# A two-block network on one core: its first transfers in smaller parts, its last sum in PSUM

## The chip, the cores and the metric

The kernel runs on one core of one Trainium2 chip. The metric is device time in microseconds (us) of one execution; the median of several runs counts. The engines are TensorE (PE in the rows, its weight loads PEld), VectorE (DVE), ScalarE (ACT), GpSimd (POOL) and SyncE (SP, which here only issues transfers; SPq and ACTq are the issuing instructions of the two queues).

## The reference, cut to what matters

Two transformer-like blocks are applied to x, which has 256 tokens of 1024 features, all in float32. The change touches the first operation and the last ones.

```python
def first_block(x, norm_mix_pre, w_in, ...):
    h = rms_norm(x, norm_mix_pre[l])
    proj = h @ w_in[l]                 # the first product: 1024 x 5376
    ...                                # attention, a delta-rule recurrence, gates, a gated FFN

def second_block(x, mem, ...):
    ...                                # a mixer and an attention over mem, each added to x
    x = x + squared_relu_mlp(rms_norm_2(x, g_mlp), w_up, w_down)   # 1024 -> 4096 -> 1024
    return rms_norm_2(x, g_final)

def squared_relu_mlp(h, w_up, w_down):
    a = jax.nn.relu(h @ w_up)
    return (a * a) @ w_down
```

`rms_norm(x, g)` is x * rsqrt(mean(x^2) + 1e-6) * g over the features.

## The kernel before

**Layout.** Activations lie feature-major: 128 partitions by 8 chunks of 256 tokens. Every large product keeps float32 accuracy by splitting both factors into a part that the matmul takes exactly (hi) and a rest (lo), and summing three products: hi*hi, hi*lo and lo*hi.

**Weights.** They stream from memory in slabs of 128 partitions by 1024 numbers (512 KB). `slab` issues one transfer on SP's queue into `wraw` (3 buffers), ScalarE copies it to `whi` (line 182) and VectorE subtracts to get `wlo` (line 183; 4 buffers each). A `wraw` buffer is free for the next transfer when that subtraction is done, so SP often stands waiting for VectorE. `plan` lists the slabs in order; `fetch(ahead)` starts slabs until so many are ready, and `next_slab` calls `fetch(AHEAD)`, with AHEAD = 3, each time TensorE takes one. One slab gives 24 matmuls of 256 columns. `block` and `group` are the loops over a 256-column group (line 247); `mm` (line 262) is the plain matmul.

**Start.** Function `first` loads x in two halves of 512 KB on SP's queue, with the first slab between them, and the small vectors `vec` on ScalarE's queue. The products of the first three groups of `w_rw` do not wait for the norm: `scaled` (lines 314 and 315) makes `gh` and `gl`, which are x times the gain without the norm, and the factor `r` = rsqrt(mean square) of each token comes in when the PSUM banks are read (`shifted`, lines 485 and 487). `rstd` makes r: squares on ScalarE (line 275), sums on VectorE (279 and 330), a matmul with ones (`ssum`), then Ln and Exp on ScalarE (line 145). All later groups use `xh` and `xl`, the normed input, which `normed` makes on VectorE and ScalarE (lines 338, 266 and 267). Constants for the attention mask (`sbf`, line 760) are loaded on ScalarE's queue and cast to bf16 (`sbm`, line 762).

**End.** Function `mlp` works on x without its norm (relu squared lets the factor out), so the product that w_down gives is scaled by r^2 of the token. `norm` makes r2 by token. `turned` transposes the gain g_final and x itself to token-major (lines 1307 and 1315) beside the up product. `tokens` multiplies token-major with 512 columns: two feature halves g, and in each the 16 slabs in order, every slab for both token halves t. Then, for each (g, t), VectorE makes y = ps * r2 + x (line 1338), ScalarE squares y with a sum (line 1340) and VectorE multiplies by the gain (1341). When both halves are there, r of the last norm is made by token and the result scaled (1350 and 1352) and written by four transfers on SP's queue (line 1353).

**Order.** The source order is a priority. A planner simulates the engines with costs of its own and fixes one order of instructions for each engine and queue; on the chip each of them goes strictly in that order. An instruction of low priority may so stand early, as a filler, where the planner expected a gap.

Of the kernel before, what the change touches and what calls it, by code (L numbers as in the profile page):

```python
# [17 lines left out]
P = 128  # L18
# [73 lines left out]
class Net:  # L92
# [47 lines left out]

    def table(self, name):
        self._chain(self.nc.scalar.preload_act_table_set(name))
# [26 lines left out]
    def fetch(self, ahead):  # L169
        while self.queue and len(self.ready) < ahead:  # L170
            name, i = self.queue.pop(0)
            self.ready.append((name, i, self.slab(name, i)))

    def slab(self, name, i):
        nc = self.nc
        off, k0, m, c0 = slabs(*WEIGHTS[name])[i]
        w = m * width(name)
        raw = self.pr.tile([P, SW], F32, tag="wraw", name="wraw")
        hi = self.ph.tile([P, SW], F32R, tag="whi", name="whi")
        lo = self.pl.tile([P, SW], F32R, tag="wlo", name="wlo")  # L180
        nc.sync.dma_start(raw[:, :w], self.io[name][off:off + P * w].rearrange("(p n) -> p n", p=P))
        nc.scalar.copy(hi[:, :w], raw[:, :w])  # L182
        nc.vector.tensor_sub(lo[:, :w], raw[:, :w], hi[:, :w].bitcast(F32))  # L183
        h3 = hi[:, :w].rearrange("p (k c) -> p k c", k=m)
        l3 = lo[:, :w].rearrange("p (k c) -> p k c", k=m)
        return h3, l3, k0, m
# [18 lines left out]
    def tokens(self, name, g, xh, xl):  # L205

        banks = [self.bank().rearrange("p c t -> p (c t)") for _ in range(2)]
        per, count = blocks(name), WEIGHTS[name][0] // P
        for b in range(per):
            hi, lo, k0, m = self.next_slab(name, g * per + b)  # L210
            for t, ps in enumerate(banks):
                tt = slice(t * P, (t + 1) * P)
                for k in range(m):
                    kk = k0 + k
                    for i, (a, w) in enumerate(((xh, hi), (xh, lo), (xl, hi))):
                        self.mm(ps, a[:, kk, tt], w[:, k, :], start=kk == 0 and i == 0,
                                stop=kk == count - 1 and i == 2)
        return banks
# [199 lines left out]
def first(n):  # L418
    nc, tc = n.nc, n.tc
    with ExitStack() as ctx:  # L420
# [15 lines left out]
        for i in range(2):  # L436
            nc.sync.dma_start(xin[i].rearrange("p c t -> p (c t)"), n.io["x"][:, i * 1024:(i + 1) * 1024])
            n.fetch(1)
        nc.scalar.dma_start(n.vec, n.io["vec"])
        n.table("natural_log_exp_and_others")  # L440
        xp = pairs(xin[0]) + pairs(xin[1])
# [4 lines left out]
        n.scaled(xp, "norm_mix_pre", gh, gl)  # L446
        r = n.rstd(tmp, xp, D, "rs")
        n.fetch(AHEAD)
# [22 lines left out]
        def shifted(g, dst, d0, scale=None, swapped=False):  # L471
            if scale is None:
                ps = n.group("w_rw", g, n.xh, n.xl)
            else:
                ps = n.group("w_rw", g, gh, gl, ps=n.sx("rw").rearrange("p (c t) -> p c t", c=2))
# [20 lines left out]
        nc.sync.dma_start(n.cst, n.io["cst"][:, :NRES])  # L496
# [263 lines left out]
        nc.scalar.dma_start(sbf, n.io["cst"][:, o:o + w])  # L760
# [529 lines left out]
def mlp(n, tmp, out):  # L1290
    nc, tc = n.nc, n.tc
    with ExitStack() as ctx:
# [3 lines left out]
        r2 = pool.tile([P, 2], F32, name="r2")  # L1296
        xt = pool.tile([P, 2, D], F32, name="xt")

        def norm():
            n.rstd_tok(pool, [n.squares(tmp, pairs(n.x))], D, square=r2)  # L1300

        def turned():

            for f in range(2):
                pt = n.ax("turn")
                for i in range(4):
                    nc.tensor.transpose(pt[:, i * P:(i + 1) * P],
                                        n.v("g_final_2", 4 * f + i).to_broadcast([P, P]), n.c("ident"))
                nc.scalar.copy(gf[:, f * 512:(f + 1) * 512], pt)
                yield  # L1310
            for t in range(2):
                for f in range(2):
                    pt = n.ax("turn")
                    for i in range(4):
                        nc.tensor.transpose(pt[:, i * P:(i + 1) * P],
                                            n.x[:, 4 * f + i, t * P:(t + 1) * P], n.c("ident"))
                    nc.scalar.copy(xt[:, t, f * 512:(f + 1) * 512], pt)
                    yield
# [15 lines left out]
        for g in range(2):  # L1334
            gg = slice(g * 512, (g + 1) * 512)
            for t, ps in enumerate(n.tokens("w_down_2", g, ah, al)):
                y = xt[:, t, gg]
                nc.vector.scalar_tensor_tensor(y, ps, r2[:, t:t + 1], y, op0=ALU.mult, op1=ALU.add)
                sq = tmp.tile([P, 512], F32, tag="t2", name="sq", bufs=n.t2)
                nc.scalar.activation(sq, y, AF.Square, accum_out=st[:, t, g:g + 1])  # L1340
                nc.vector.tensor_mul(o[:, t, gg], y, gf[:, gg])
        for t in range(2):
            s = st[:, t, :]
            nc.vector.tensor_add(s[:, 2:3], s[:, 0:1], s[:, 1:2])
            n.act(s[:, 3:4], s[:, 2:3], AF.Ln, bias=n.eps, scale=1.0 / D)
            n.act(s[:, 3:4], s[:, 3:4], AF.Exp, scale=-0.5)
            for f in range(2):
                oo = o[:, t, f * 512:(f + 1) * 512]
# [4 lines left out]
                nc.sync.dma_start(out[t * P:(t + 1) * P, f * 512:(f + 1) * 512], oo)  # L1353
# [85 lines left out]
```

## Time and profile before

| | |
|---|---|
| median of 3 runs | 851.95 us (851.76 to 854.29) |
| profiled execution, its own time | 853.44 us |
| its span, first to last instruction | 851.7 us |
| mean granted TensorE clock | 0.994 of full speed |
| TensorE busy | 829.5 us, 97% of the span |
| VectorE busy | 565.3 us, 66% |
| ScalarE busy | 464.9 us, 55% |
| moved by transfers | 142.88 MB, 168 GB/s over the span |

Line numbers (L247) are lines of the kernel before. In a timeline row the first number is the start and the second the duration in us; "x4" are instructions merged into one row; in square brackets stands how long the engine was idle before it and what ended that. A busy TensorE is not one at its peak, as matmuls are pipelined: what one costs is read from the distance between starts.

### The profile page before, as it was taken

The numbers are of one execution on the slowest core, as the hardware profiler recorded it, in microseconds if no ns is written. First come the engines' busy times: TensorE is split into PE (matmuls) and PEld (weight loads), VectorE is DVE, ScalarE is ACT, GpSimd is POOL, SyncE is SP. The second block draws the span as 40 slices with busy tenths as digits, with TensorE's granted clock in tenths as the row PEclk, the third lists the DMA queues.
The fourth block names the chain that finished last, engine by engine and source line by source line (L and its number), as shares of the span: only waits on it lengthen the run. The fifth ranks groups of instructions, "written<-read, shape, count | busy, mean of one in ns | idle before, by whom it ended". The sixth has DMA issues, their size and how long they took to land.

```text
span 851.7 us, 15759 instructions
## 1 busy us (share of the span) xinstructions
PE 829.5 (97%) x6508; PEld 788.4 (93%) x6508; DVE 565.3 (66%) x790; ACT 464.9 (55%) x714; POOL 5.4 (1%) x14
## 2 busy tenths in 40 slices
PE   5999998999999999999999999999999999999996
PEld 5798987999999999999999998999999999988884
DVE  6858689455888776666545876689576666654543
ACT  6497355643577654445445657457455565553432
POOL 0001001000000000000000000000000000000000
PEclk9999999999999999999999999999999999999999
DMA  8434443542464765555555564455524555556551
GB/s 283 149 133 159 136 130 117 160 140 87 145 251 144 225 189 183 195 177 197 173 187 186 158 202 149 148 174 184 188 95 153 176 172 177 193 178 193 179 193 50
DMA packets 44631, 142.88 MB, mean 168 GB/s; under 512 B 8976, under 2 KB 9744, under 8 KB 44304
## 3 DMA queue, kind: packets, MB, share of 16 engines
q1 hardware_dynamic: 43840, 139.25, 50.7%
q10 hardware_dynamic: 720, 2.63, 0.8%
q8 instruction: 51, 0.84, 0.4%
q14 instruction: 20, 0.16, 0.1%
HBM read 139.17 MB, written 2.69 MB: 167 GB/s over the span
## 4 chain that ended last, share of the span: by engine, by line
PE 90%; DVE 5%; DMA 2%; ACT 2%; issue 1%; SPq 0%; ACTq 0%; DVEq 0%
PE mm L247 68%; PE mm L262 11%; DMA wraw<-in_w_rw 2%; PE pz L262 2%; DVE wlo L183 1%; PE po L262 1%; ACT whi L182 1%; PE px L262 1%; PE mgnh L262 1%; PE nv L262 1%; DVE prw L736 1%; PE kv L247 1%; PE ssum L262 1%; DVE pr L718 1%; DVE TF L719 0%
## 5 line engine op out<-in xcount | busy, mean ns | idle before, releaser
L183 DVE TENSOR_TENSOR wlo<-wraw,whi 128x1024 fp32r<-128x1024 f32 x254 | 308.2, 1215 | 198.8 <-ACT whi L182 197.3
L182 ACT CAST whi<-wraw 128x1024 fp32r<-128x1024 f32 x254 | 264.8, 1044 | 291.5 <-PE mm L247 174.9
L247 PE MATMUL mm<-xh,whi 128*128 128x256 f32 x1120 | 319.3, 285 | 0.0
L247 PE MATMUL mm<-xh,wlo 128*128 128x256 f32 x1120 | 316.1, 282 | 1.8 <-DVE wlo L183 1.8
L247 PE MATMUL mm<-xl,whi 128*128 128x256 f32 x1120 | 316.1, 282 | 0.0
L247 PEld LDWEIGHTS mm<-xh,whi 128*128 128x128 f32 x1120 | 212.0, 189 | 3.8 <-issue 2.2
L247 PEld LDWEIGHTS mm<-xh,wlo 128*128 128x128 f32 x1120 | 211.8, 189 | 2.9 <-DVE wlo L183 2.2
L247 PEld LDWEIGHTS mm<-xl,whi 128*128 128x128 f32 x1120 | 211.8, 189 | 0.9 <-issue 0.7
L262 PE MATMUL mm<-whi,ah 128*128 128x512 f32 x128 | 50.6, 395 | 0.0
L262 PE MATMUL mm<-whi,al 128*128 128x512 f32 x128 | 50.6, 395 | 0.0
L262 PE MATMUL mm<-wlo,ah 128*128 128x512 f32 x128 | 50.6, 395 | 0.0
L247 PE MATMUL mm<-fh,whi 128*128 128x256 f32 x176 | 49.1, 279 | 0.0
L247 PE MATMUL mm<-fl,whi 128*128 128x256 f32 x176 | 49.1, 279 | 0.0
L247 PE MATMUL mm<-fh,wlo 128*128 128x256 f32 x176 | 49.1, 279 | 0.0
L247 PEld LDWEIGHTS mm<-fl,whi 128*128 128x128 f32 x176 | 33.1, 188 | 0.0
L247 PEld LDWEIGHTS mm<-fh,wlo 128*128 128x128 f32 x176 | 33.1, 188 | 0.0
L247 PEld LDWEIGHTS mm<-fh,whi 128*128 128x128 f32 x176 | 33.1, 188 | 0.0
L262 PEld LDWEIGHTS mm<-whi,al 128*128 128x128 f32 x128 | 24.1, 188 | 5.8
L262 PEld LDWEIGHTS mm<-wlo,ah 128*128 128x128 f32 x128 | 24.1, 188 | 5.8
L262 PEld LDWEIGHTS mm<-whi,ah 128*128 128x128 f32 x128 | 24.1, 188 | 5.7
L247 PE MATMUL rw<-gh,whi 128*128 128x256 f32 x48 | 14.2, 296 | 9.0 <-ACT whi L182 9.0
L247 PE MATMUL mm<-memh,whi 128*128 128x256 f32 x64 | 18.8, 294 | 0.0
(349 smaller groups left out, 1379.9 us busy)
## 6 DMA issues: line engine op xcount, KB each, us to landing
wraw<-in_w_up SPq DMA_DIRECT2D x32, 512.0 KB, 3.5
wraw<-in_w_down SPq DMA_DIRECT2D x32, 512.0 KB, 4.3
wraw<-in_w_in SPq DMA_DIRECT2D x24, 512.0 KB, 4.2
wraw<-in_w_ffn_gate SPq DMA_DIRECT2D x22, 512.0 KB, 3.8
wraw<-in_w_ffn_up SPq DMA_DIRECT2D x22, 512.0 KB, 3.3
wraw<-in_w_ffn_down SPq DMA_DIRECT2D x20, 512.0 KB, 3.5
wraw<-in_w_gate SPq DMA_DIRECT2D x16, 512.0 KB, 3.3
wraw<-in_w_kv_mem SPq DMA_DIRECT2D x16, 512.0 KB, 3.3
```

What stands on the lines that cost most here:

```text
L182: nc.scalar.copy(hi[:, :w], raw[:, :w])
L183: nc.vector.tensor_sub(lo[:, :w], raw[:, :w], hi[:, :w].bitcast(F32))
L247: self.nc.tensor.matmul(ps[:, c, :], lhsT, rhs, start=first, stop=last, skip_group_check=True)
L262: self.nc.tensor.matmul(out, lhsT, rhs, start=start, stop=stop, skip_group_check=True)
L718: nc.vector.tensor_mul(pr[:, :, :, :t + 1], tri[:, :, :, :t + 1], q)
L736: nc.vector.tensor_mul(pr, left[:, r:r + 4, :].rearrange("p r (o i) -> p r o i", o=1).to_broadcast([P, 4, 16, 16]), right.rearrange("p (o ...
```

## The change

It has two halves. **At the start**, x comes in three transfers on two queues (256 KB on SP's, then 256 KB and 512 KB on ScalarE's, behind `vec`), the first slab comes in two transfers with its copies in two parts, TensorE multiplies ones by ones 12 times into a bank that nobody reads, and the source order is changed: a quarter of x, the first slab, the second quarter, the second slab, the rest of x, the third slab, the first product group, and only then `rstd`. The mask constants go on SP's queue, behind `cst`. **At the end**, the residual is summed by TensorE in the banks of the last product. As a norm follows, the sum may be scaled by token: x * ms + f, with ms = mean(x^2) + eps, replaces x + f * r^2, and the last norm's eps is scaled by ms^2. So x is multiplied by ms in place (four VectorE instructions), `norm` has one more matmul, the transposes of x and line 1338 are gone, and `residual` adds 16 float32 matmuls against the identity, four to each bank, ahead of the bank's slabs. In the second feature half the last two slabs are held back and gone through by token half, and the output leaves on two queues.

```diff
-    def fetch(self, ahead):
+    def fetch(self, ahead, parts=1):
...
+        cols = [slice(q * w // parts, (q + 1) * w // parts) for q in range(parts)]
+        for c in cols:
+            nc.sync.dma_start(raw[:, c], src[:, c])
+        for c in cols:
+            nc.scalar.copy(hi[:, c], raw[:, c])
+            nc.vector.tensor_sub(lo[:, c], raw[:, c], hi[:, c].bitcast(F32))
...
-    def tokens(self, name, g, xh, xl):
+    def tokens(self, name, g, xh, xl, first, hold=0):
...
+        for t, ps in enumerate(banks):
+            first(g, t, ps)
+
+        def part(slab, t):
+            hi, lo, k0, m = slab
+            tt = slice(t * P, (t + 1) * P)
+            for k in range(m):
+                kk = k0 + k
+                for i, (a, w) in enumerate(((xh, hi), (xh, lo), (xl, hi))):
+                    self.mm(banks[t], a[:, kk, tt], w[:, k, :], start=False, stop=kk == count - 1 and i == 2)
+
+        for b in range(per - hold):
+            slab = self.next_slab(name, g * per + b)
+            for t in range(2):
+                part(slab, t)
+        held = [self.next_slab(name, g * per + b) for b in range(per - hold, per)]
+        for t in range(2):
+            for slab in held:
+                part(slab, t)
...
-        for i in range(2):
-            nc.sync.dma_start(xin[i].rearrange("p c t -> p (c t)"), n.io["x"][:, i * 1024:(i + 1) * 1024])
-            n.fetch(1)
         nc.scalar.dma_start(n.vec, n.io["vec"])
+        for i, (queue, q) in enumerate(((nc.sync, 0), (nc.scalar, 2), (nc.scalar, 4))):
+            w = 2 if i < 2 else 4
+            dst = xin[q // 4][:, q % 4:q % 4 + w, :].rearrange("p c t -> p (c t)")
+            queue.dma_start(dst, n.io["x"][:, q * T:(q + w) * T])
         n.table("natural_log_exp_and_others")
+
+        idle = n.ax("idle")
+        for i in range(12):
+            n.mm(idle[:, :P], n.ones, n.ones)
...
-        n.scaled(xp, "norm_mix_pre", gh, gl)
+        n.scaled(xp[:1], "norm_mix_pre", gh, gl)
+        n.fetch(1, parts=2)
+        n.scaled(xp[1:2], "norm_mix_pre", gh, gl, 1)
+        n.fetch(2)
+        n.scaled(xp[2:], "norm_mix_pre", gh, gl, 2)
+        n.fetch(AHEAD)
+        rw = {}
+
+        def raw_group(g):
+            rw[g] = n.group("w_rw", g, gh, gl, ps=n.sx("rw").rearrange("p (c t) -> p c t", c=2))
+
+        raw_group(0)
         r = n.rstd(tmp, xp, D, "rs")
-        n.fetch(AHEAD)
...
-        nc.sync.dma_start(n.cst, n.io["cst"][:, :NRES])
+        cst = nc.sync.dma_start(n.cst, n.io["cst"][:, :NRES])
...
-        nc.scalar.dma_start(sbf, n.io["cst"][:, o:o + w])
+        n.after(nc.sync.dma_start(sbf, n.io["cst"][:, o:o + w]), cst)
...
         def norm():
-            n.rstd_tok(pool, [n.squares(tmp, pairs(n.x))], D, square=r2)
+            sq = n.squares(tmp, pairs(n.x))
+            ps, pr = n.ax("ssum"), n.ax("rtok")
+            n.mm(ps[:, :T], n.ones, sq)
+            for t in range(2):
+                n.mm(pr[:, t:t + 1], sq[:, t * P:(t + 1) * P], n.ones[:, 0:1], start=t == 0)
+            nc.vector.tensor_scalar(ms, ps[:, :T], 1.0 / D, EPS, op0=ALU.mult, op1=ALU.add)
+            nc.vector.tensor_scalar(epsm, pr[:, :2], 1.0 / D, EPS, op0=ALU.mult, op1=ALU.add)
+            nc.vector.scalar_tensor_tensor(epsm, epsm, EPS, epsm, op0=ALU.mult, op1=ALU.mult)
+            for x in pairs(n.x):
+                nc.vector.tensor_mul(x, x, pair(ms))
...
-            for t in range(2):
-                for f in range(2):
-                    pt = n.ax("turn")
-                    for i in range(4):
-                        nc.tensor.transpose(pt[:, i * P:(i + 1) * P],
-                                            n.x[:, 4 * f + i, t * P:(t + 1) * P], n.c("ident"))
-                    nc.scalar.copy(xt[:, t, f * 512:(f + 1) * 512], pt)
-                    yield
+
+        def residual(f, t, ps):
+            for i in range(4):
+                n.mm(ps[:, i * P:(i + 1) * P], n.x[:, 4 * f + i, t * P:(t + 1) * P], n.c("ident"),
+                     start=i == 0)
...
-            for t, ps in enumerate(n.tokens("w_down_2", g, ah, al)):
-                y = xt[:, t, gg]
-                nc.vector.scalar_tensor_tensor(y, ps, r2[:, t:t + 1], y, op0=ALU.mult, op1=ALU.add)
+            for t, ps in enumerate(n.tokens("w_down_2", g, ah, al, residual, hold=2 * g)):
                 sq = tmp.tile([P, 512], F32, tag="t2", name="sq", bufs=n.t2)
-                nc.scalar.activation(sq, y, AF.Square, accum_out=st[:, t, g:g + 1])
-                nc.vector.tensor_mul(o[:, t, gg], y, gf[:, gg])
+                nc.scalar.activation(sq, ps, AF.Square, accum_out=st[:, t, g:g + 1])
+                nc.vector.tensor_mul(o[:, t, gg], ps, gf[:, gg])
...
-            n.act(s[:, 3:4], s[:, 2:3], AF.Ln, bias=n.eps, scale=1.0 / D)
+            n.act(s[:, 3:4], s[:, 2:3], AF.Ln, bias=epsm[:, t:t + 1], scale=1.0 / D)
...
-                nc.sync.dma_start(out[t * P:(t + 1) * P, f * 512:(f + 1) * 512], oo)
+                (nc.sync if f else nc.scalar).dma_start(out[t * P:(t + 1) * P, ff], oo)
```

## Rows read from the trace of the kernel before

**Rows 1.** The page, part 1: busy time of each engine over the span.

```profile
PE 829.5 (97%) x6508; PEld 788.4 (93%) x6508; DVE 565.3 (66%) x790; ACT 464.9 (55%) x714; POOL 5.4 (1%) x14
```

**Rows 2.** Waits of TensorE, whole span: in total, times, longest, us.

```profile
PE rw L247 <- ACT whi L182: 9.0, 1, 9.0
...
PE mm L247 <- DVE wlo L183: 1.8, 1, 1.8
```

**Rows 3.** Busy time by stretch; last columns: granted clock, DMA share, GB/s.

```profile
23.00:33.00 10.00, 8.51 (x61) 6.94 (x59) 9.58 (x18) 5.59 (x9) 0.00 (x0) 1.00 0.34 106
...
756.00:842.70 86.70, 86.70 (x373) 69.88 (x372) 38.68 (x35) 31.19 (x33) 0.00 (x0) 1.00 0.51 160
```

**Rows 4.** Timeline of VectorE, start of the kernel.

```profile
6.55 1.68 DVE L315 SCALAR_TENSOR_TENSOR gl<-x,vec,gh 128x256 fp32r<-128x256 f32 x4 [0.29 <-ACT gh L314]
...
8.96 1.23 DVE L183 TENSOR_TENSOR wlo<-wraw,whi 128x1024 fp32r<-128x1024 f32 x1 [0.73 <-ACT whi L182]
...
15.95 0.42 DVE L330 TENSOR_TENSOR sqa<-sqa 128x256 f32<-128x256 f32 x1
...
18.15 0.49 DVE L485 SCALAR_TENSOR_TENSOR wx<-rw,omu,rs 128x256 f32<-128x256 f32 x1 [0.65 <-ACT rs L145]
...
23.17 1.22 DVE L183 TENSOR_TENSOR wlo<-wraw,whi 128x1024 fp32r<-128x1024 f32 x1 [1.23 <-ACT whi L182]
...
30.18 1.90 DVE L267 TENSOR_TENSOR xl<-nh,xh 128x512 fp32r<-128x512 f32 x3 [0.24 <-ACT xh L266]
32.00 2.35 DVE L183 TENSOR_TENSOR wlo<-wraw,whi 128x1024 fp32r<-128x1024 f32 x2
```

**Rows 5.** Timeline of ScalarE, start of the kernel.

```profile
6.01 1.70 ACT L314 ACTIVATE gh<-x,vec 128x256 fp32r<-128x256 f32 x4 [3.55 <-DMA vec<-in_vec]
7.88 1.04 ACT L182 CAST whi<-wraw 128x1024 fp32r<-128x1024 f32 x1 [0.17 <-DMA wraw<-in_w_rw]
...
15.44 0.51 ACT L762 CAST sbm<-sbf 128x384 bf16<-128x384 f32 x1
...
17.19 0.47 ACT L145 ACTIVATE lg<-ssum,eps 128x256 f32<-128x256 f32 x1 [1.05 <-PE ssum L262]
```

**Rows 6.** Single microseconds of the start, columns as in rows 3.

```profile
4.00:5.00 1.00, 0.00 (x0) 0.00 (x0) 0.00 (x0) 0.00 (x0) 0.00 (x0) 1.00 0.91 241
...
10.00:11.00 1.00, 0.76 (x3) 0.76 (x4) 1.00 (x3) 1.00 (x3) 0.00 (x0) 1.00 0.42 168
11.00:12.00 1.00, 1.00 (x7) 1.00 (x6) 1.00 (x4) 1.00 (x3) 0.00 (x0) 1.00 0.78 184
...
18.00:19.00 1.00, 1.00 (x11) 1.00 (x11) 0.85 (x3) 0.98 (x2) 0.00 (x0) 1.00 0.93 340
...
34.00:35.00 1.00, 1.00 (x6) 1.00 (x6) 1.00 (x3) 0.00 (x0) 0.00 (x0) 0.50 0.67 147
```

**Rows 7.** The chain that ended last, in order of time: pieces of TensorE.

```profile
45.07 1.73 PE gpre L262 x8
46.80 1.78 PE cum L262 x16
...
690.23 0.44 PE turn L1315 x4
```

**Rows 8.** Timeline of the last microseconds, VectorE, ScalarE and SP's queue.

```profile
844.11 0.75 DVE L1338 SCALAR_TENSOR_TENSOR xt<-mm,r,xt 128x512 f32<-128x512 f32 x1
...
844.90 0.63 ACT L1340 ACTIVATE sq<-xt 128x512 f32<-128x512 f32 x1 [0.67 <-DVE xt L1338]
...
845.95 0.28 ACT L145 ACTIVATE fst<-fst,eps 128x1 f32<-128x1 f32 x1
...
846.74 0.19 ACT L145 ACTIVATE fst<-fst 128x1 f32<-128x1 f32 x1
846.96 0.72 ACT L1352 ACTIVATE o<-o,fst 128x512 f32<-128x512 f32 x1
...
846.59 1.96 SPq L1353 DMA_DIRECT2D out<-o  x4
```

More of the change, by code (lines that the diff above doesn't have):

```diff
@@ L139, in _chain, with after @@
         self.last_table = ins.ins
+    def after(self, ins, other):
+        self.tc.add_manual_dep(
+            ins.ins, other.ins.name,
+            mybir.DependencyInfo(mybir.DependencyClass.NoSync, mybir.DependencyReason.DATA),
+            reason="transfers in order")
     def table(self, name):
@@ L167, in plan_together, with slab @@
             self.queue += [(name, g * blocks(name) + b) for name, g in groups]
-    def fetch(self, ahead):
+    def fetch(self, ahead, parts=1):
         while self.queue and len(self.ready) < ahead:
             name, i = self.queue.pop(0)
-            self.ready.append((name, i, self.slab(name, i)))
-    def slab(self, name, i):
+            self.ready.append((name, i, self.slab(name, i, parts)))
+    def slab(self, name, i, parts=1):
         nc = self.nc
@@ L180, in slab @@
         lo = self.pl.tile([P, SW], F32R, tag="wlo", name="wlo")
-        nc.sync.dma_start(raw[:, :w], self.io[name][off:off + P * w].rearrange("(p n) -> p n", p=P))
-        nc.scalar.copy(hi[:, :w], raw[:, :w])
-        nc.vector.tensor_sub(lo[:, :w], raw[:, :w], hi[:, :w].bitcast(F32))
+        src = self.io[name][off:off + P * w].rearrange("(p n) -> p n", p=P)
+        cols = [slice(q * w // parts, (q + 1) * w // parts) for q in range(parts)]
[4 more added lines that the diff above has]
+            nc.vector.tensor_sub(lo[:, c], raw[:, c], hi[:, c].bitcast(F32))
         h3 = hi[:, :w].rearrange("p (k c) -> p k c", k=m)
@@ L203, in together @@
         return banks
-    def tokens(self, name, g, xh, xl):
+    def tokens(self, name, g, xh, xl, first, hold=0):
         banks = [self.bank().rearrange("p c t -> p (c t)") for _ in range(2)]
         per, count = blocks(name), WEIGHTS[name][0] // P
[L209 to L217, printed above, removed]
+        for t, ps in enumerate(banks):
[15 more added lines that the diff above has]
+                part(slab, t)
         return banks
@@ L474, in shifted @@
             else:
-                ps = n.group("w_rw", g, gh, gl, ps=n.sx("rw").rearrange("p (c t) -> p c t", c=2))
+                if g not in rw:
+                    raw_group(g)
+                ps = rw[g]
             t = pad[g % 2]
@@ L1295, in mlp @@
         gf = pool.tile([P, D], F32, name="gf")
-        r2 = pool.tile([P, 2], F32, name="r2")
-        xt = pool.tile([P, 2, D], F32, name="xt")
+        ms = pool.tile([P, T], F32, name="ms")
+        epsm = pool.tile([P, 2], F32, name="epsm")
         def norm():
-            n.rstd_tok(pool, [n.squares(tmp, pairs(n.x))], D, square=r2)
+            sq = n.squares(tmp, pairs(n.x))
[8 more added lines that the diff above has]
+                nc.vector.tensor_mul(x, x, pair(ms))
         def turned():
@@ L1344, in mlp @@
             nc.vector.tensor_add(s[:, 2:3], s[:, 0:1], s[:, 1:2])
-            n.act(s[:, 3:4], s[:, 2:3], AF.Ln, bias=n.eps, scale=1.0 / D)
+            n.act(s[:, 3:4], s[:, 2:3], AF.Ln, bias=epsm[:, t:t + 1], scale=1.0 / D)
             n.act(s[:, 3:4], s[:, 3:4], AF.Exp, scale=-0.5)
             for f in range(2):
-                oo = o[:, t, f * 512:(f + 1) * 512]
+                ff = slice(f * 512, (f + 1) * 512)
+                oo = o[:, t, ff]
                 if f:
```

## The prediction

> **What bounds the kernel now.** I read the page first. TensorE is busy for 829.5 of 851.7 us [rows 1], so an edit can win only in the few stretches where TensorE stands, and whatever it adds to TensorE elsewhere is paid in full. The view of TensorE's waits says where it stands [rows 2]: 9.0 us until the first slab is copied, and 1.8 us for a `wlo`; to these comes the tail behind its last matmul. The change works at exactly these places: at the first two with its first half, at the tail with the first part of its second half.
>
> Next come the stretches of the start. From 23 to 33 us VectorE is busy for 9.58 of 10 us, TensorE for 8.51 [rows 3]. The timeline of VectorE shows why. It starts on `gl` at 6.55, and the `wlo` for which TensorE waits is the first of the two that start at 32.00; two take 2.35 us, so it is there at about 33.2 [rows 4]. In the 26.65 us between, VectorE waits only four times: 0.73, 0.65, 1.23 and 0.24 us [rows 4], 2.85 us together. The other 23.8 us are work, mostly without a gap. So the start is not bound by TensorE, and not by the transfers alone: it is a queue of 23.8 us of VectorE's work that must be gone through before the first product of the normed input can go on. The reader should keep this ledger in mind: the stage ends at (VectorE's first `gl`) + 23.8 + (its waits).
>
> In the last product TensorE has no gap at all, 86.70 of 86.70 us [rows 3].
>
> **The change part by part: the start.** The first `gh` waits 3.55 us for `vec` and begins at 6.01 [rows 5]. Ahead of it on the queues were 512 KB of x and the 73 KB of `vec`; now it is 256 KB and 73 KB. The engines moved 241 GB/s at that time [rows 6], so 256 KB less is about 1.06 us. I put the first `gl` at 5.4 instead of 6.55. If the landing is fixed time and not bytes, the gain is 0; if the smaller transfers also land in their turn with less overlap, it may be 1.6.
>
> The first slab's copy began at 7.88, by the landing of its transfer [rows 5]. Its first half now stands behind 256 KB on SP's queue, with the second quarter of x beside it: some 840 KB must land where it was about 1.2 MB (two times 512 KB, `vec` and half of `sbf`). That is 360 KB less, 1.1 to 1.5 us by 340 to 241 GB/s [rows 6], so about 6.7. A half copy is half of 1.04 us [rows 5], and VectorE, which ends its two first `gl` (half of 1.68 us [rows 4]) at 6.25, waits until about 7.35: 1.1 us. The second half and the second half of x land together at about 8.8, the second slab at about 10; the squares and their first sum can fill one of these waits, as they do not need the weights. I count one more of 0.45 us. Further on, r is made from the squares as before: the last sum was at 15.95 and r was used at 18.15 [rows 4], 2.2 us of which VectorE filled all but 0.65 with a `wlo`. In the new source order r has a lower priority than the third slab; I count 0.6. The wait of 1.23 us is for the copy of a slab that landed late, as SP had issued it only when a `wraw` was free; the transfers had dips such as 0.42 of the engines at 10 to 11 us [rows 6] for that reason. Buffers come free earlier now, and I take this wait as gone. Last, 0.25 as before. The waits sum to 1.1 + 0.45 + 0.6 + 0.25 = 2.4 us.
>
> The ledger is then 5.4 + 23.8 + 0.1 (two halves of a subtraction instead of one) + 2.4 = 31.7, against 33.2 before: 1.5 us less; I take **1.4**. Its bounds: first `gl` at 5.0 and waits of 1.0 give 29.9, a gain of 3.3; first `gl` at 6.5 and waits of 4.0 give 34.4, a loss of 1.2.
>
> The 12 products of ones cost nothing: TensorE does nothing in the first 9.0 us [rows 2]. Their record form, 128 by 128 against 128 columns, is that of `cum`: 16 records in 1.78 us [rows 7], two for each product, 0.22 us each. Twelve take 2.7 us, or 5.3 at half the clock, over by about 6.5; the first real matmul comes at about 7.4. What they give is speed in the first microseconds of the real work: from 11 to 12 us 7 matmuls were in work, from 18 to 19 us 11 [rows 6]. It buys nothing at the end of the stage while VectorE ends last there. [...]
>
> Moving `sbf` to SP's queue takes 192 KB out of the first microseconds and puts one issue more (a quarter of 1.96 us for four [rows 8]) among SP's waits: 0 in the sum, with a rival below.
>
> From 33 us on TensorE is the bound, so what is won at the first normed product stays won. The half clock of 0.50 at 34 to 35 us [rows 6] follows a stand of TensorE; I keep it in the sum, as TensorE will stand there again.
>
> **The change part by part: the end.** TensorE loses 16 transposes of x: four pieces such as the one of 0.44 us for four [rows 7], 1.76 us. It gains 16 float32 products of the form of `cum`, 0.1113 us for a record and two records each [rows 7]: 3.56 us. And one `ssum` of 256 columns, the form of `gpre`: 1.73 us for 8 records, four products [rows 7], 0.43 us. The sum is -1.76 + 3.56 + 0.43 = **+2.2 us**, in stretches without a gap. Nothing is there to hide it, as the products open each bank. Bounds: 1.4 if a record in this stream costs a quarter less, 4 if it costs half more.
>
> The new VectorE work (four multiplications of 128x512, at most 0.75 us each as in line 1338 [rows 8], and three small ones) is about 3.5 us beside up products whose slabs are ready three ahead. The slabs of the last product pass in 86.7 us for about 32, 2.7 us each [rows 3], so the lead is some 8 us: 0 in the sum. Without that lead up to 3.5 us would be paid. Line 1338 and four ScalarE copies go; they were not on the path except in the tail.
>
> The tail: the last bank is read at 844.11, by 0.75 us of line 1338, and the square starts at 844.90 [rows 8]. Now the square reads the bank: -0.79. Its Ln ends at 846.23, but Exp starts only at 846.74, behind the scaling of the other token half on ScalarE [rows 8]: -0.51, as the first half is through 12 matmuls before the end (86.7 us for 384 are 0.226 each, so 2.7 us) and not 6. The last scaling so ends at 847.68 - 1.30 = 846.38 and not 847.68 [rows 8]. The four issues on SP ended at 848.55 [rows 8]; the last two now go from two queues, so the last ends at about 846.38 + 0.49 = 846.87, 1.7 us earlier, and the first half's 512 KB have left before them. I take **-1.8**, with bounds of 1.3 (the transfers do not overlap better) and 2.1.
>
> **The sum.** -1.4 + 2.2 - 1.8 = -1.0 us. The profiled execution has a span of 851.7 and a time of 853.44, 1.7 us around it; I expect a span of 850.7. The median of the runs is 851.95, so the forecast is **850.9 us**, a change that the measurement hardly tells from none: 0.3% is 2.56 us, about what can be told for this kernel.
>
> **The rivals.**
> - *The first transfers are hidden anyway* (the change does not do what it says). VectorE waits later what it does not wait now, and the stage ends at 33.2 as before. For it: 23.8 of 26.65 us there are work, whatever lands when. Time: 851.95 + 2.2 - 1.8 = 852.35.
> - *The waits of VectorE nearly go and TensorE does not stand any more* (faster). The stage ends at 29.9, 3.3 us earlier: 851.95 - 3.3 + 0.4 = 849.05; if TensorE also keeps its clock, which was 0.50 at 34 to 35 us [rows 6], half a microsecond more for each such one, and three of them would make 847.6. For it: the wait is only 1.8 us long. Against it: the ledger leaves 1 us of waits in all, with three landings before the first nine microseconds are over.
> - *A cast holds up ScalarE* (slower). `sbm` stood at 15.44 among ScalarE's work, ahead of the Ln at 17.19 which makes r [rows 5]. Its input now comes on SP's queue, behind `cst` and behind whatever waits of SP stand there. If the planner leaves the cast in its place and the transfer lands later than about 17.2, r, the next copies of slabs and VectorE's whole rest come later by the same time; from a landing at about 20.8 the kernel is slower by over 0.3%. At 22 it is 850.9 + 4.8 = 855.7. Against it: `cst` itself was there in time, and the planner sees the new queue.
> - *Smaller transfers are slow* (no gain at the start). [...] As a mechanism of this kernel: the rate at 4 to 5 us, 241 GB/s [rows 6], would not hold for the smaller pieces, the first slab would land no earlier, and the time is that of the first rival, 852.4. I count it there.
>
> **How the numbers follow.** Forecast case (849.4 to 852.0) 0.40; hidden anyway 0.24; faster 0.25; slower 0.11. The first two are within 0.3%, with a hundredth more or less at their edges. So faster 0.26, same 0.62, slower 0.12. The range goes from 848.2 (most of the faster case) to 854.0 (the first rival with residual products that cost half more).
>
> **What would show it.** In the changed profile: the first `gl` at about 5.4; the first `rw` matmul at about 7.4 instead of 9.0 [rows 2]; the first normed product's wait ends near 31.7; r used at about 18; the records of `residual` 32, at 0.11 us from start to start, and the last product's stretch longer by 3.6 us; from the last matmul to the end of the span 5.8 us instead of 7.6. Wrong I am if the planner's order behind 33 us is another one, if VectorE stands for under 1 us in all, or if `sbm` stalls ScalarE.

## The result, and the profile after

The changed kernel takes **857.49 us** in the median of 20 runs (852.70 to 863.36), the kernel before 852.50 beside it (20 runs, 850.87 to 854.29): a ratio of **1.0063, 95% interval 1.0042 to 1.0084**. It is slower, and outside the range of 848.2 to 854.0.

One thing must be known to read the numbers: the executions of one kernel lie further apart after the change than before, and, with few exceptions, they lie in the order of TensorE's mean granted clock. Nine runs of the changed kernel in the first experiment go from 852.99 and 853.07 us at a clock of 0.997 over 857.41 at 0.991 to 861.66 and 861.87 at 0.984 and 0.983. A straight line through these nine falls by 0.64 us for each 0.001 of the clock, one through the 21 runs of the kernel before beside them by 0.66. The profiled execution below is one of the first kind: 852.86 us, with a span of 851.1.

The page, busy time: TensorE has 5.2 us more than in [rows 1].

```profile
PE 834.7 (98%) x6550; PEld 793.4 (93%) x6550; DVE 565.7 (66%) x794; ACT 464.5 (55%) x708; POOL 5.4 (1%) x14
```

TensorE's waits, whole span (in total, times, longest). The 9.0 us for the first slab and most of the 1.8 us for `wlo` [rows 2] are gone. New are the wait for `lora` and the one of `apre`; the one of `pz` for `zm` was 2.7 us in the kernel before, too (second fence).

```profile
PE pz L284 <- DVE zm L823: 2.7, 1, 2.7
PE wraw L284 <- DMA lg<-in_lora: 2.5, 1, 2.5
...
PE apre L284 <- ACT a L152: 0.6, 1, 0.6
PE mm L269 <- DVE wlo L194: 0.4, 1, 0.4
```

```profile
PE pz L262 <- DVE zm L784: 2.9, 2, 2.7
```

ScalarE's timeline at the start (compare [rows 5]). `gh` starts at 4.76 instead of 6.01. But each of the squares (L297) now stands behind a copy of a slab (L193), one of these copies behind 1.62 us of waiting for its transfer, and the Ln that makes r comes at 24.52 where it was at 17.19. `sbm` passes at 18.73 without a wait.

```profile
4.76 0.91 ACT L336 ACTIVATE gh<-x,vec 128x256 fp32r<-128x256 f32 x2 [1.33 <-DMA vec<-in_vec]
6.14 0.62 ACT L193 CAST whi<-wraw 128x512 fp32r<-128x512 f32 x1 [0.48 <-DMA wraw<-in_w_rw]
...
17.25 1.05 ACT L193 CAST whi<-wraw 128x1024 fp32r<-128x1024 f32 x1 [1.62 <-DMA wraw<-in_w_rw]
18.20 0.63 ACT L297 ACTIVATE sq<-x 128x512 f32<-128x512 f32 x1
18.73 0.50 ACT L801 CAST sbm<-sbf 128x384 bf16<-128x384 f32 x1
19.14 1.05 ACT L193 CAST whi<-wraw 128x1024 fp32r<-128x1024 f32 x1
20.19 0.63 ACT L297 ACTIVATE sq<-x 128x512 f32<-128x512 f32 x1
...
24.52 0.48 ACT L152 ACTIVATE lg<-ssum,eps 128x256 f32<-128x256 f32 x1 [0.47 <-PE ssum L284]
```

VectorE's timeline: the first `gl` at 5.30 (6.55 in [rows 4]), the first use of r at 25.48 (18.15).

```profile
5.30 0.88 DVE L337 SCALAR_TENSOR_TENSOR gl<-x,vec,gh 128x256 fp32r<-128x256 f32 x2 [0.29 <-ACT gh L336]
...
18.33 1.23 DVE L194 TENSOR_TENSOR wlo<-wraw,whi 128x1024 fp32r<-128x1024 f32 x1 [1.55 <-ACT whi L193]
...
25.48 0.49 DVE L524 SCALAR_TENSOR_TENSOR wx<-rw,omu,rs 128x256 f32<-128x256 f32 x1 [0.17 <-ACT rs L152]
```

SP's queue: six slab transfers are issued between 14.72 and 25.66, each when a `wraw` comes free, and `lora` behind them at 25.71. It was issued at 16.44 before (second fence).

```profile
14.72 10.94 SPq L191 DMA_DIRECT2D wraw<-in_w_rw  x6
25.71 0.43 SPq L536 DMA_DIRECT2D lg<-in_lora  x1
```

```profile
16.44 0.42 SPq L497 DMA_DIRECT2D lg<-in_lora  x1
```

TensorE's timeline: it stands from 28.4 until `lora` lands at 30.96, and reaches the first normed product at 32.84, from where there is no gap until 40 us. In the kernel before (second fence) four normed products ran first and the next ones started at 33.27.

```profile
30.96 0.66 PE L284 MATMUL wraw<-lg,wx 64*128 64x512 f32 x1 [2.51 <-DMA lg<-in_lora]
...
32.84 0.50 PE L269 MATMUL mm<-xh,whi 128*128 128x256 f32 x2
```

```profile
33.27 0.49 PE L247 MATMUL mm<-xh,wlo 128*128 128x256 f32 x1 [1.76 <-DVE wlo L183]
```

The first products of the slabs: after the products of ones those of the changed kernel start 0.12 us apart (first fence) until TensorE waits at 8 to 9.8, and 0.21 us apart from there to 13.1. Those of the kernel before (second fence) start 0.21 us apart until 12.8.

```profile
7.76 0.28 PE L269 MATMUL rw<-gh,whi 128*128 128x256 f32 x1
7.88 0.28 PE L269 MATMUL rw<-gl,whi 128*128 128x256 f32 x1
```

```profile
10.62 0.41 PE L247 MATMUL rw<-gh,whi 128*128 128x256 f32 x1
10.84 0.41 PE L247 MATMUL rw<-gl,whi 128*128 128x256 f32 x1
```

Stretches of this execution, columns as in [rows 3]; the third figure from the end is the granted clock. At 10 to 14 us it is 0.61: it reads 0.50 from 10 to 13 us, where the products start 0.21 us apart, and 1.00 behind 14. In the kernel before the same column reads 1.00 at 10 to 14 us although the products start 0.21 us apart until 12.8, too: the column does not show the slow products with which that execution begins, and there the distance of the products decides. The last fence is the kernel before at 28 to 32 us.

```profile
10.00:14.00 4.00, 4.00 (x23) 4.00 (x24) 3.36 (x7) 3.94 (x8) 0.00 (x0) 0.61 1.01 375
28.00:32.00 4.00, 1.49 (x9) 0.88 (x9) 4.00 (x10) 2.45 (x4) 0.00 (x0) 1.00 0.47 166
32.00:40.00 8.00, 7.64 (x55) 6.35 (x53) 8.00 (x17) 4.03 (x8) 0.00 (x0) 1.00 0.01 3
138.00:148.00 10.00, 10.00 (x76) 8.55 (x75) 8.85 (x11) 5.97 (x8) 1.91 (x2) 1.00 0.50 139
```

```profile
28.00:32.00 4.00, 3.51 (x18) 1.94 (x17) 3.75 (x9) 2.61 (x4) 0.00 (x0) 1.00 0.00 1
```

The end: groups of TensorE's instructions (busy time, mean ns of one), then ScalarE's timeline and VectorE's. The 32 records of the residual are there; the 16 of the first feature half start from 750.87 on, and the next product at 752.57, 1.70 us later. In the tail, the square of the second token half starts at 844.66 on the bank itself, but `o` of the same bank waits for the square and ends at 846.07, and `fst` stands behind it.

```profile
L284 PE MATMUL mm<-cst,x 128*128 128x128 f32 x32 | 3.9, 275 | 0.0
```

```profile
750.87 1.95 PE L284 MATMUL mm<-cst,x 128*128 128x128 f32 x16
752.57 0.48 PE L284 MATMUL mm<-whi,ah 128*128 128x512 f32 x1
```

```profile
844.26 0.35 ACTq L1399 DMA_DIRECT2D out<-o  x1
844.66 0.60 ACT L1385 ACTIVATE sq<-mm 128x512 f32<-128x512 f32 x1 [0.43 <-ACT o L1398]
```

```profile
845.38 0.69 DVE L1386 TENSOR_TENSOR o<-mm,gf 128x512 f32<-128x512 f32 x1 [1.39 <-ACT sq L1385]
845.99 0.15 DVE L1389 TENSOR_TENSOR fst<-fst 128x1 f32<-128x1 f32 x1
```

### The profile page after: what moved, and what is told of

Same layout as the page of the kernel before. It is cut to its first block, busy times and chain, and to the rows that moved or that the text cites. A ratio compares the mean times of both kernels' runs of the same rounds, so it can differ in the third digit from the quotient of the medians.

```text
span 851.1 us, 15850 instructions
## 1 busy us (share of the span) xinstructions
PE 834.7 (98%) x6550; PEld 793.4 (93%) x6550; DVE 565.7 (66%) x794; ACT 464.5 (55%) x708; POOL 5.4 (1%) x14
## 4 chain that ended last, share of the span: by engine, by line
PE 90%; DVE 4%; DMA 2%; ACT 2%; issue 1%; SPq 0%; ACTq 0%; DVEq 0%
PE mm L269 68%; PE mm L284 11%; DMA wraw<-in_w_rw 2%; PE pz L284 2%; DVE wlo L194 1%; PE po L284 1%; PE px L284 1%; PE mgnh L284 1%; ACT whi L193 1%; PE nv L284 1%; DVE prw L775 1%; PE kv L269 1%; PE ssum L284 1%; DVE pr L757 1%; DMA lg<-in_lora 1%
## 5 line engine op out<-in xcount | busy, mean ns | idle before, releaser
L194 DVE TENSOR_TENSOR wlo<-wraw,whi 128x1024 fp32r<-128x1024 f32 (+1 forms) x255 | 308.7, 1211 | 201.4 <-ACT whi L193 200.6
L193 ACT CAST whi<-wraw 128x1024 fp32r<-128x1024 f32 (+1 forms) x255 | 264.8, 1040 | 290.4 <-PE mm L269 175.3
L269 PE MATMUL mm<-whi,xh 128*128 128x256 f32 x64 | 18.4, 288 | 0.0
```

Source lines behind the costliest of these rows:

```text
L193: nc.scalar.copy(hi[:, c], raw[:, c])
L194: nc.vector.tensor_sub(lo[:, c], raw[:, c], hi[:, c].bitcast(F32))
L269: self.nc.tensor.matmul(ps[:, c, :], lhsT, rhs, start=first, stop=last, skip_group_check=True)
```

## The experiments

**The changed kernel again, its halves, and without the ones.** The same file, to see the trace of another execution; then each half alone (`tokens` and `mlp` of one kernel put into the other); then without the products of ones.

```diff
 # e2: the changed kernel with
-            for t, ps in enumerate(n.tokens("w_down_2", g, ah, al, residual, hold=2 * g)):
+            for t, ps in enumerate(n.tokens("w_down_2", g, ah, al)):
 # e3: the kernel before with that line the other way round
 # e4: the changed kernel with
-        for i in range(12):
-            n.mm(idle[:, :P], n.ones, n.ones)
```

> The changed kernel once more, as it is. Its runs lie between 852.7 and 863.4 us with mean granted clocks from 0.997 down to 0.983, while those of the kernel before lie within 850.9 to 854.3. Every theory expects the same spread here, in groups near 853, 857 and 861, the time rising by some 4 us for each 0.006 of the mean clock. A profile of a slow execution would show where TensorE has the clock 0.50; one near 853 would not.

> The first half of the change alone (smaller first transfers, products of ones, new source order; the end as before). Theory 1, the start loses the clock: TensorE is released by the ones, has thin work from 6.5 to 10 us and falls to 0.50, in some executions for longer; then this kernel spreads as the whole change does, median 4 to 6 us over the kernel before. Theory 2, the end loses it: this kernel is steady, 2 us under the kernel before (849.5 to 851).

> The second half alone (residual by TensorE, held slabs, two output queues; the start as before). Theory 1, the start loses the clock: steady, +2.2 us of TensorE's work and -1.3 us in the tail, 852.5 to 853.5. Theory 2, the float32 products against the identity or the new order at the end lose the clock: it spreads up to 861, median 4 to 6 us over the kernel before.

> The whole change without the 12 products of ones. If the ones are what sets off the loss of clock (they release TensorE early, and its thin work from 6.5 to 10 us then has it gated again), the spread is gone and the median is 851 to 853. If another part does it, the spread stays, and the first matmuls are slow as in the kernel before: within 1 us of the whole change.

Against 851.77 of the kernel before: again 859.1 (ratio 1.0078, 1.0054 to 1.0103), the start alone 860.46 (1.0093, 1.0070 to 1.0117), the end alone **852.9 (1.0015, 1.0004 to 1.0027)**, without ones 858.7 (1.0075, 1.0047 to 1.0103). So the end costs about 1.1 us, the start nearly all else, and the ones are neither its cause nor of use to the time. Stretches of the changed kernel run again (span 857.0), as above:

```profile
10.00:14.00 4.00, 4.00 (x22) 4.00 (x23) 3.43 (x7) 4.00 (x8) 0.00 (x0) 0.57 1.00 384
28.00:32.00 4.00, 1.44 (x8) 0.79 (x7) 4.00 (x11) 2.49 (x4) 0.00 (x0) 0.81 0.55 201
32.00:40.00 8.00, 8.00 (x40) 5.97 (x38) 8.00 (x17) 2.25 (x4) 0.00 (x0) 0.67 0.01 3
138.00:148.00 10.00, 7.61 (x32) 5.61 (x33) 9.33 (x9) 2.94 (x5) 1.91 (x2) 0.66 0.42 124
```

The stands are nearly those of the execution above (`lora` 2.6, `zm` 2.7, `apre` 1.1 us), but now the clock goes to 0.50 behind the first and the last (32 to 36 and 140 to 146 us). The rows of the first `pz` behind the last stand, in the execution above and in this one:

```profile
137.36 2.00 PE L284 MATMUL pz<-zm,cst 128*128 128x384 f32 x8 [2.67 <-DVE zm L823]
```

```profile
140.39 3.78 PE L284 MATMUL pz<-zm,cst 128*128 128x384 f32 x8 [2.69 <-DVE zm L823]
```

This execution is 3.0 us late there and 5.9 us late at the last of these `pz` products (154.7 instead of 148.8), and it stays so up to the first residual product (756.83 instead of 750.87): all that it loses is lost by the end of the stretch behind that stand. The loss of clock is 0.19 x 4 + 0.33 x 8 + 0.34 x 10 = 6.8 us of full clock, less what TensorE would have stood anyway; the spans differ by 5.9.

**What is late: r or lora?** The source order is put back in part: r made ahead of the third slab (e5), `lora` and `g_up` loaded ahead of the first products (e6), both (e7). In e8 the wait stays, and 11 products that nothing reads fill it.

```diff
+        r = n.rstd(tmp, xp, D, "rs")      # e5, e7
         n.fetch(AHEAD)
+        nc.sync.dma_start(lora, n.io["lora"])   # e6, e7; g_up too
...
+        warm = n.ax("warm")               # e8, ahead of the wraw products
+        for i in range(11):
+            n.mm(warm[:, :P], n.ones[0:64, :], xs[0:64, 0, 0:P])
```

> The whole change, but with rstd back in its old place of the source order (ahead of the third slab and of the first product group). In the changed kernel the squares stand behind slab copies on ScalarE and r comes at 25.5 instead of 18.2 us. Theory A, the late r is the root of TensorE's new stands at 28 to 31 and 42 to 45 us, after which the clock falls to 0.50: r comes at about 18 again, the stands shrink to 1 us or less, the spread goes and the median is 850 to 852. Theory B, the late transfer of lora (issued at 25.7, behind ten slabs) is the root: it stays late, and the median stays at 857 to 860.

> The whole change, with only the transfers of lora and g_up put ahead of the first product group, so that they leave at about 5 us. Theory B (lora is the root): TensorE goes from the last rw matmul into the small products without a stand, and the median is 850 to 853. Theory A (late r is the root): the small products need the tanh of the first shifted group, which ends at 28.6 us as r is late, and after them the normed input at 31.5; the stand is only shortened from 2.5 to 1 or 1.5 us, and the times still spread, median 854 to 858.

> Both together: rstd in its old place and lora early. By theory A and by theory B alike the stand at 28 to 31 us goes and the median is 850 to 852; if this kernel still spreads like the whole change, neither is the root, and the stands at 42 to 45 or at 136 us would have to carry the loss alone.

> The whole change with 11 more products of ones (against the tanh output, so that they cannot start before 28.6 us, some 2.4 us of them) in the stand at 28 to 31 us; nothing reads them, and every wait is where it was. If the loss is the clock and not the waits, the clock at 31 to 38 us stays at 1.00, and the median falls by about half of the loss, by 3 us to 855 to 856 (the other stands remain). If the waits themselves cost the time, the median stays at 857 to 860 or grows by up to 0.5.

These four ran on another chip than e1 to e4, each beside the kernel before; the changed kernel as it is was not run there. Against 851.87: r early **854.62 (1.0032, 1.0021 to 1.0044)**, lora early 856.7 (1.0063, 1.0047 to 1.0079), both 854.94 (1.0037, 1.0023 to 1.0050), the fill 854.93 (1.0038, 1.0021 to 1.0054). r early gives back about half of the loss (0.0032 is left of the 0.0063 and 0.0078 above), lora alone little: without its wait TensorE stands for `wlo` and `xh` instead (2.0 and 0.8 us). Both give no more than r alone, where 850 to 852 was expected; TensorE then stands 3.3 us for `wlo`. With r early the Ln is at 21.41, not yet at 17.19, and `lora` goes out at 19.97. But the fill, which removes no wait, gives as much as r early. In its profile, that of its slowest run, the clock is still 0.58 at 32 to 40 us, behind 0.9 us of the wait that the fill left open. The intervals of r early and of the fill touch that of the first measurement of the changed kernel, so the half is a rough figure.

**All stands filled, and the tail alone.** To decide between the clock and the waits, fills for all three stands of the changed kernel (e9) and both of the kernel before (e10); in the kernel before also the last blocks by token half and the two output queues alone (e11), and both (e12).

```diff
+            if j == 0:                     # e9, e10, e12: behind the first po
+                warm = n.sx("warm")
+                for _ in range(11):
+                    n.mm(warm[:, :P], n.ones, wt[:, 0, 0:P])
...
-                nc.sync.dma_start(out[...], oo)       # e11, e12
+                (nc.sync if f else nc.scalar).dma_start(out[...], oo)
```

> The changed kernel with idle products put into three stands of TensorE, none of them read by anything: 11 of 128 by 128 by 128 ahead of the lora product (the stand at 28 to 31 us), 5 between the two halves of apre (42 to 44), 11 behind the first po (137 to 140). The waits themselves stay. Theory 1 (the loss is TensorE's clock, which falls to 0.50 after these stands): no fall at 32 to 39 and at 140 to 147 us, the mean clock over 0.996, and a time of 851.5 to 853.5, what the quick executions of the changed kernel take; runs over 857 go away. Theory 2 (the waits are the loss, the lower clock only goes with it): 857 to 859 as before the filling.

> The kernel before, with idle products in its two stands: 7 behind the wraw products (31.5 to 33.3 us, before the late wlo) and 11 behind the first po (134 to 137 us). Theory 1 (stands cost by the clock that falls after them): the profile before shows 0.50 for some 4 us after each, about 1.9 us of time for each; without the falls 849 to 850.5 in the median, a ratio of 0.997 to 0.999, and a narrower spread than 850 to 854. Theory 2 (the waits alone cost): no change, 851.5 to 852.5, as both waits still end when they ended.

> The kernel before with only the order of the last blocks by token half and the outputs on two queues; the turned residual, its transposes and line 1338 stay. By the prediction's tail (1.8 us less, of which the 0.79 of line 1338 stays here): about 1.0 us less, 850.5 to 851.3. If the tail is held by the scaling and the output issue on ScalarE's queue instead: 0 to 0.5 less, 851.4 to 852.2.

> The two edits to the kernel before together: idle products in its two stands, and the last blocks by token half with outputs on two queues. By theory 1 and the tail as predicted: 848 to 849.8, a ratio of 0.996 to 0.998, below both kernels. By theory 2: only the tail's part, 850.5 to 852.

Against 851.6: e9 859.81, e10 856.3, e11 **850.82 (0.9988, 0.9976 to 1.0001)** and e12 856.23. One fill misses in all three kernels that have it: TensorE stands behind the second `po`, not the first. Behind the first, TensorE's timeline of e9 shows 2.7 us of added work without a stand, and then a stand of 3.85 us instead of 2.7:

```profile
126.29 2.72 PE L284 MATMUL warm<-ab,ones 128*128 128x128 f32 x22
...
142.36 3.63 PE L284 MATMUL pz<-zm,cst 128*128 128x384 f32 x8 [3.85 <-DVE zm L830]
```

The tail edit alone gives 0.8 us (by the interval, 2.0 less to 0.1 more), near the 1.0 that is left of my 1.8 when line 1338 stays.

**The fills in the right place, and a stand made on purpose.** e13 and e14 are e9 and e10 with 10 products behind the second `po`. In e15 to e17 the kernel before gets copies on GpSimd between the tanh and the `wraw` products: 2, 4 and 16. e18 is e14 with the tail.

```diff
-            if j == 0:                     # e13, e14, e18
+            if j == 1:
...
+        nc.gpsimd.tensor_copy(xw[0][0:64, :], xs[0:64, 0, :])      # e15 to e17
+        for i in range(k - 1):
+            nc.gpsimd.tensor_copy(xw[1 - i % 2][0:64, :], xw[i % 2][0:64, :])
```

> As the filling of all stands of the changed kernel, but with the third fill (10 products) behind the second po, where the stand of 2.7 us is. The one before missed it: its third fill stood behind the first po, was paid in full (2.7 us) and left the stand. In its profile the first two fills did hold the clock at 1.00 from 14 to 142 us. Theory 1 (the loss is TensorE's clock, which falls after stands): no fall behind 14 us in most executions and 852 to 853.5. Theory 2 (the waits alone): 856 to 859.

> The kernel before with 7 idle products in its stand at 31.5 to 33.3 us and 10 behind the second po. The one before showed no fall at 33 to 37 us, but paid 2.7 us for a fill in the wrong place. Theory 1: 849.5 to 851, ratio 0.997 to 0.9995, and fewer executions over 853. Theory 2: no change, 851.5 to 852.5.

> The kernel before with the input of the wraw products passed through two copies on GpSimd, which is idle there: TensorE stands ahead of wraw for about 1 to 2.5 us, and nothing else is moved. Theory 1: the clock falls to 0.50 after the stand in most executions, and the time grows by more than the stand, about 2 us for the fall, less what the later wait for wlo (1.8 us) takes back: 852 to 854.5. Theory 2: the stand only moves the wait for wlo forward, and the time stays within 0.5 us of before.

> The same with four copies, a stand of about 2.5 to 5 us. Theory 1: a fall that lasts longer or comes in every execution, some 2 to 3 us more than what the stand costs beyond the wait for wlo that it replaces: 855 to 858, and executions as far apart as those of the changed kernel. Theory 2: the stand's length less 1.8 us, 852.5 to 855, with executions no further apart than before.

> The kernel before with 16 copies on GpSimd between the tanh and the wraw products: by 0.47 us for a copy from 24.0 us on they end at about 31.4, so TensorE stands from 28.9 to 31.4, as it does in the changed kernel, and the later wait for wlo nearly goes. Theory 1 (a stand there is followed by a fall of the clock, more often than in the kernel before): the profile shows 0.50 at 32 to 38 us, the mean clock of the runs is lower by some thousandths, 853 to 856. Theory 2: only the work behind the stand comes later, by some 0.3 to 0.8 us: 852 to 852.6.

> The kernel before with both fills in the right places and the last blocks by token half with outputs on two queues. The two edits gave 0.65 and 0.8 to 1.0 us less alone; added: 850.0 to 850.5, a ratio of 0.9975 to 0.9988, below both kernels. If the tail's part is lost or shared: 851.

The changed kernel, filled (e13): 855.91 against 851.8 (1.0055, 1.0040 to 1.0069), with its runs between 855.42 and 858.42 at clocks of 0.995 to 0.999. The runs over 859 are gone, but so are those at 853. The profile has no fall behind 14 us; its span is 853.6, 2.5 over the one of the execution above, with the first `pz` behind the stand at 138.98 instead of 137.36: the fills are work and partly outlast the stands. My 852 to 853.5 was too low by that much, and 855.91 is no lower than the time of e8, which fills one stand only. Its slowest run, 858.42, has a clock of 0.997, so something else than the recorded clock slows that one.

The kernel before, filled (e14): 851.15 against 851.8 (**0.9991, 0.9982 to 0.9999**), between 850.42 and 851.96; unfilled it goes from 849.78 to 853.3. The two falls of its profile, 0.21 x 8 and 0.17 x 10 us in the first of these two fences (the kernel before), are not in the second (e14):

```profile
32.00:40.00 8.00, 6.73 (x39) 6.26 (x40) 7.99 (x12) 3.35 (x5) 0.00 (x0) 0.79 0.44 136
138.00:148.00 10.00, 10.00 (x64) 8.57 (x65) 8.86 (x9) 4.54 (x6) 1.92 (x2) 0.83 0.42 111
```

```profile
32.00:40.00 8.00, 8.00 (x55) 6.48 (x54) 8.00 (x12) 3.40 (x5) 0.00 (x0) 1.00 0.40 135
138.00:148.00 10.00, 10.00 (x77) 8.54 (x76) 8.85 (x11) 6.14 (x9) 1.92 (x2) 1.00 0.52 140
```

Two and four copies made no stand: they were done before the products came, and the times, 851.36 and 851.61, are those of before; these two runs tell nothing of stands. Sixteen did: TensorE stood for 3.36 us ahead of `wraw`, the wait for `wlo` went, and the time is **857.1 against 851.72 (1.0064, 1.0050 to 1.0078)**, the ratio of the changed kernel. Its clock is 0.991 to 0.994 where that of before is 0.995 to 0.998. The row of `wraw` in TensorE's timeline, and the stretches:

```profile
32.03 0.69 PE L262 MATMUL wraw<-lg,xw 64*128 64x512 f32 x1 [3.36 <-POOL xw L513]
```

```profile
32.00:40.00 8.00, 7.97 (x42) 6.36 (x43) 8.00 (x12) 2.88 (x5) 0.00 (x0) 0.79 0.43 131
138.00:148.00 10.00, 8.64 (x51) 7.01 (x52) 8.86 (x10) 4.20 (x6) 1.92 (x2) 0.83 0.40 121
```

So one stand there, with what the copies do besides, costs as much as the whole change. It is not the clock alone: this execution has the two falls of before, no longer ones, and its span is 1.8 us longer, as the products behind `wraw` are later; the runs at a clock of 0.991 take another 2 us. VectorE is also slower beside GpSimd's copies (six `nh` in 3.29 us instead of 2.46, last section), so this run is no clean measure of the stand's own price.

e18 takes **850.33 against 851.72 (0.9985, 0.9976 to 0.9994)**, between 849.80 and 851.19, with a clock of 0.997 to 0.999: 1.4 us below the kernel before, and the lowest median and ratio of all.

## Why the prediction was wrong

Two steps failed at the start, one in the tail; the runs suggest that the two of the start are linked. In the order of the prediction:

- *First gl at 5.4, first product at 7.4*: 5.30 and 6.81. The first slab's copy starts at 6.14 instead of 7.88: the smaller transfers do land earlier, and the rival of slow small transfers is out.
- *The ones cost nothing and speed up the first products*: both hold. The ones are 5.38 us of work, done at 6.55, and the first products behind them start 0.12 us apart instead of 0.21. TensorE was then busy for 2.4 of the 4 us from 6 to 10, and the products from 9.8 to 13.1 start 0.21 us apart again; in the profiles of e2 and e8 they don't (31 and 29 records at 10 to 14 us, where the first profile of the changed kernel has 23, and a clock of 1.00). Without the ones (e4) there are 19 in these 4 us, 0.21 us for each. The speed buys nothing at the end, as I had said: the time of e4 is that of e1.
- *r used at about 18, for 0.6 us of waiting* (**the step that failed first**). I saw that r had a lower priority than the third slab and priced that by VectorE's wait. VectorE did wait only 0.17 us for r, as `wlo` work filled the time. What I left out is who comes behind r: r at 25.48 instead of 18.15 moves `wx`, the tanh, `xh` and, as e5 shows, `lora`'s issue. TensorE, which had run out of raw products at 28.4, met them with nothing else to do.
- *The stage ends 1.4 us earlier*: the first normed product runs from 32.84 without a gap. Before, four products ran ahead of the gap and the rest from 33.27, which is worth 33.27 - 4 x 0.117 = 32.80. The gain is 0, as in the rival "hidden anyway"; but that rival has VectorE's queue as the bound, and here TensorE stood for `lora`. VectorE's waits from the first `gl` to there are 4.7 us where I counted 2.4, the largest the 1.55 us shown. Then come the waits for `wlo` at 40 us and of `apre`, 0.4 and 0.6 us. At the same clock the start half costs 1.0 us: the first residual product of the changed kernel starts at 750.87, that of the end half alone at 749.83, both without a fall behind 14 us.
- *The half clock stays in the sum as it was* (**the step that cost most**). I saw the stand and the fall that follows it, and assumed one of the same price. In the kernel before TensorE was busy for 3.51 + 6.73 of the 12 us from 28 to 40; in the changed one for 1.49 + 7.64, even in the execution shown. In the trace of e1 TensorE then runs for longer at the lower clock (0.67 at 32 to 40 us, where the kernel before has 0.79) and again behind 138 us (0.66 against 0.83); the mean clocks of 21 of the changed kernel's 29 runs are 0.983 to 0.993, those of the kernel before 0.994 to 0.998.
  That the longer stand makes the falls longer is not proven: the fill in e8, with the same late values and ready products in the stand, takes 854.93, and e17, with a stand put in, 857.1, but e13 shows no gain beyond e8, and in e17 GpSimd's copies disturb.
  The number of slow first products varies as well: some 15 from 9.8 to 13.1 us in the first profile of the changed kernel, none in that of e8, which has the same start. The falls behind the stands vary too, 1.00 and 0.67 at 32 to 40 us behind the same stand, and no run here shows what decides it.
- *The base of the sum.* I made it against the profiled span of 851.7, which holds two falls worth up to 0.21 x 8 + 0.17 x 10 = 3.4 us. The changed kernel's profiled execution has none of them and is at 851.1: the likeness to my 850.7 is chance, two errors that cancel.
- *+2.2 us of TensorE at the end*: the two groups of residual records take 1.70 us each, 3.4 of the 3.56 that I counted, and the end half and the tail alone differ by 1.0015 - 0.9988, 2.3 us (by their intervals, some 1.5 us either way). Right.
- *Tail -1.8*: from the last matmul's end (844.20) to the end of the span it is 6.9 us, before 7.6: -0.7. The edit of order and queues gives that alone (6.9 us in e11, too). The 0.79 us of line 1338 did not come: the square starts 0.46 us behind the last matmul, as the output issue on ScalarE's own queue lasts until 844.61, and the program lets `o` wait for the square of the same bank, with `fst` behind it. With line 1338 (e11) `fst` starts 0.75 us after the square does; here it is 1.33.
- *sbm stalls ScalarE*: it didn't. r came late, as that rival feared, but because its squares stood behind the copies of slabs.

At the same clock the change costs 1.0 + 2.2 - 0.7 = 2.5 us; the quickest runs are 1.8 to 2.8 apart. The other half of the 5 us, or more, goes with the clock. What stays open: whether the longer stand is what makes the falls longer, why a fall follows the same stand in one execution and not in another, and which of the later falls (138 us) comes of the start. Smaller transfers with the order of before were not tried alone.

## What to carry to other kernels

When an edit lets an engine start earlier, follow the value that the next stage needs (here r) through every queue it passes, and price its delay by what the slowest engine does when its own work runs out, not by the wait of the engine that reads it first. In these kernels a gap in TensorE's work cost its length and what the clock did behind it (1.00 in one execution, 0.67 over 8 us in another, behind the same 2.5 us), so compare the granted clock of several executions, and judge a sum against an execution whose falls are known. With idle products that wait for nothing late, about as long as two gaps of the kernel before and exactly there, the clock read 1.00 behind both (e14), where it had read 0.79 and 0.83; 2.7 us of them in the wrong place (e10) cost 4.7 us, more than its two falls.

## What the runs showed of the hardware

- The same 2.7 us stand at 134 to 140 us is followed by a clock of 0.83 over 10 us in the kernel before, and by 1.00 in the first profile of the changed one and 0.66 in its second.
- The price of a fall: where the granted clock read 0.50 (34 to 36 us), the 128x256 products of the kernel before started 0.214 us apart, and where it read 1.00 behind that (37 to 38.4 us), 0.118.
- VectorE was slower beside GpSimd's copies. In e17, whose 16 ran from 21.93 to 31.98, the operation `k<-k,pad` on 128x512 took 0.88 us beside them (26.02) and 0.68 behind them (36.88). Six `nh` took 3.29 us beside them, 0.55 each; without them, in the same view of the kernel before (second fence), 2.46, 0.41 each:

```profile
26.83 3.29 DVE L338 SCALAR_TENSOR_TENSOR nh<-x,vec,rs 128x256 f32<-128x256 f32 x6
```

```profile
27.48 2.46 DVE L338 SCALAR_TENSOR_TENSOR nh<-x,vec,rs 128x256 f32<-128x256 f32 x6
```
